# A two-layer trunk in float32r: first transfers, late head norms, a gate tile of its own, a residual in three steps, and one query panel copied out of PSUM

## The chip, the cores and the metric

The kernel runs on one core of one Trainium2 chip. The metric is the device time of one execution in microseconds; lower is better. Three runs of the kernel before took 2197.4, 2202.26 and 2202.55 us, median 2202.26. One execution was profiled: it took 2199.56 us, and its span, first to last recorded instruction, is 2197.8 us.

## The reference

256 tokens of width 2048 go through two layers. Everything is float32.

```python
h = x
u = rms_norm(h, g_a);  q, k, v, fz = split(u @ w_in)          # 3*2048 + 16 gate columns
q, k = rms_norm per head (16 heads of 128)
c = cumsum(log_sigmoid(fz + b_f))                             # per head, over tokens
s = q k^T / sqrt(128) + c[query] - c[key],  causal;  o = softmax(s) v
h = h + o @ w_out
h = h + relu(rms_norm(h, g) @ w1)**2 @ w2                     # 2048 -> 8192 -> 2048
k, v = split(rms_norm(h, g_kv) @ kv_w);  k = rms_norm per head   # shared, computed once
q = rms_norm per head of rms_norm(h, g_b) @ w_q
o = softmax(q k^T / sqrt(128) + relative bias, chunks of 64) v
h = h + o @ w_out
h = h + relu(rms_norm(h, g) @ w1)**2 @ w2
```

## The kernel before

**Weights.** All weight products use float32r. A weight is split into a high part and a remainder, `w = hi + lo` (L142 on ScalarE, L143 on VectorE), the activations likewise, and three products are summed: high by high, high by low, low by high (L319 to L321). The weights come in *units* of 128 x 1024 float32, 512 KB each, which is two contraction blocks of 128 rows by 512 output columns. With two blocks of 128 tokens a unit makes 2 x 2 x 3 = 12 matmuls. Eight units make a *panel*: 512 output columns of all 256 tokens, gathered in a pair of PSUM banks. `ps_acc` holds two such pairs.

The 768 units come in this order: 0 to 95 the input projection (for each of four head groups a q, a k and a v panel), 96 to 127 the output projection, 128 to 383 the MLP in four chunks of hidden columns, 384 to 415 the second layer's q, 416 to 479 the shared k and v, 480 to 511 its output projection, 512 to 767 its MLP. Where a stage is *woven*, its first two panels take turns unit by unit, so that a block of the activations late in the row is needed twice as late.

**Order.** `panels` (L323) runs over the eight units: `fetch` gives a split unit and keeps two more split ahead and up to three raw ones on the way; then come the 12 matmuls; then `run_fill` runs one item of a list named `fill`; and after the last unit the panel's `evac` functions follow, one for each token block. So everything beside the weights is cut into steps, and each step is given a *slot*: the unit after which it is written. `add_fill(items)` adds its n-th item to the n-th slot from now. `keep_order` then fixes the written order on VectorE, ScalarE, TensorE and SyncE, so that a step that waits holds up all that is written behind it on its engine. GpSimd is left free. All transfers are issued by SyncE. A transfer also waits for the one eight before it, since eight semaphores go round among them.

**Turning a panel.** A panel's result has tokens on the partitions, the next product wants them in the free dimension. `blocks32` transposes 32 x 32 blocks on VectorE (L208), and `carry` (L211) puts the rest into DRAM traffic: one store of the rows (`turn<-z`), one empty slot, then four transfers of columns back. Its users: `head_norm`, which squares the accumulator on ScalarE (L347), sums on VectorE (L349), takes a power on GpSimd (L353) and scales out of PSUM on VectorE (L357) before the turn; `turn_hidden` in the MLP, whose `take` does the squared ReLU and the split of one quarter of the hidden activations (L568 to L575); and `next_x`.

**Residual.** `next_x` (L232) ends a panel of an output projection or of the MLP's last chunk. In the evac itself it adds the panel to h on VectorE (L376 or L378), squares the new h on ScalarE with a row sum (`stats.add`, L274), and leaves the turn for the next slot and the carry for the one after; then two steps scale and split the next x (`split_turned`, L188 to L192). These *transitions* lie at 358 to 416 us, 1058 to 1119 us and 1444 to 1506 us. The row statistics are finished by `inverse`, `both` or `flip`, each given a slot after the last panel. The second transition goes to the second layer's q (stage at 1108), and `again` builds a second x in reversed token order for the shared k and v.

**Start.** `begin` (L456) loads x block by block before each of the first panel's units, splits it, loads 8 blocks of h (4 pairs) and squares them, and takes the row roots at the last unit; before the second unit it loads the head gains `hgb` and scales them (L466 to L469). The k panel's slots then hold the two turns of the q panel, `spread` (L295: the row factors as a 128 x 256 tile, by two small matmuls), and `gates` (L482): two steps that each take a buffer of the weight pool's `hi`, clear it on GpSimd (L492), fill it (L495, L496) and make 8 matmuls (L499), then the logs (L503), their store to DRAM and a transpose of the sums. The attention of the group waits for the bias made from that store, for q's columns and for k's; its scores come in the eighth slot of the v panel.

Of the kernel before, what the change touches and what calls it, by code (L numbers as in the profile page):

```python
# [15 lines left out]
P = 128  # L16
# [4 lines left out]
H = 16  # L21
# [26 lines left out]
def trunk(ctx: ExitStack, tc: tile.TileContext, xT, xr, gs, hg, bf, wgate, w_in, w_oa, w1a, w2a,  # L48
# [28 lines left out]
    load_x(0)  # L77
    gsb = const.tile([P, 5 * KT], F32, name="gsb")
    SY.dma_start(gsb, gs)

# [10 lines left out]
    V.memset(mhalf, -0.5)  # L91
    hgb = const.tile([P, 4], F32, name="hgb")
# [139 lines left out]
    def next_x(n, r2, stats, which, into, kept=None):  # L232
# [14 lines left out]
        def f(b, ps):  # L247
            add_h(b, ps)
            stats.add(b, n)
            if b == NB - 1:  # L250
                step = steps(use)
                add_fill([[turn], [lambda: add_fill(carry(*zt) + [[step], [step]])]])
                if kept is not None:
                    kept.append(use)
# [12 lines left out]
    class RowStats:  # L267
# [27 lines left out]
        def spread(self):  # L295
            self.R = const.tile([P, T], F32, name="R")
            pr = ps_o.tile([P, 512], F32, name="pt", tag="po")
            for b in range(NB):
                rb = wk.tile([P, P], F32, name="rb", tag="wk")
                V.tensor_scalar(rb, ones[:, :P], self.r[:, b : b + 1], None, op0=ALU.mult)  # L300
                TE.matmul(pr[:, b * P : (b + 1) * P], rb, ident, start=True, stop=True)
            V.tensor_copy(self.R, pr[:, :T])

# [38 lines left out]
    def head_norm(stats, z, dst):  # L342
        rns = []

        def f(b, ps):
            sq = wk.tile([P, 512], F32, name="sq", tag="wk")
# [3 lines left out]
            vv = sm.tile([P, GH], F32, name="vv")  # L350
            V.tensor_scalar(vv, ss, 1.0 / P, stats().e[:, b : b + 1], op0=ALU.mult, op1=ALU.add)  # L351
            rn = sm.tile([P, GH], F32, name="rn")
            G.tensor_tensor(rn, vv, mhalf, op=ALU.pow)  # L353

            def turn():
                qn = wk.tile([P, 512], F32, name="qn", tag="wk")
                V.tensor_tensor(qn.rearrange("p (a d) -> p a d", a=GH), ps.rearrange("p (a d) -> p a d", a=GH),  # L357
# [3 lines left out]
            rns.append(turn)  # L361
            if b == NB - 1:
                add_fill([[t] for t in rns] + carry(z, dst))
# [57 lines left out]
    def attend(g, q, k, v, cq, o, make_bias, gap):  # L421
# [5 lines left out]
        items[1].append(step)  # L427
        items[4].append(step)
        items[5].append(step)
        for a in range(GH):  # L430
# [25 lines left out]
    def begin(u):  # L456
# [8 lines left out]
        if u == 1:  # L465
            SY.dma_start(hgb, hg)  # L466
            SY.dma_start(bfb, bf)
            V.tensor_scalar(gqk, hgb[:, 0:2], float(P) ** -0.5, None, op0=ALU.mult)
            V.tensor_tensor(gqk, gqk, hgb[:, 2:4], op=ALU.mult)  # L469
        if 2 <= u < 6:  # L470
            for b, n in chunks[2 * u - 4 : 2 * u - 2]:
                c = slice(n * 512, (n + 1) * 512)
                SY.dma_start(h[b][:, c], xr[b][:, c])
        if 4 <= u:
            for b, n in chunks[2 * u - 8 : 2 * u - 6]:
                st0.add(b, n)
        if u == KT // UA - 1:
            st0.roots()

    ct = {}  # L480

    def gates(x, st):  # L482
        wgr = const.tile([P, KT * H], F32, name="wgr")
        r3 = wgr.rearrange("p (k c) -> p k c", k=KT)
        ps = []
        UG = UN // P

        def products(u):
            if u == 0:
                ps.append(ps_s.tile([P, 512], F32, name="s"))  # L490
            w = wsp.tile([P, UN], F32R, name="hi")
            G.memset(w.bitcast(F32), 0.0)  # L492
            w3 = w.rearrange("p (k c) -> p k c", k=UG)
            h3, l3 = w3[:, :, :H], w3[:, :, 32 : 32 + H]
            S.activation(h3, r3[:, u * UG : (u + 1) * UG, :], AF.Copy)  # L495
            V.tensor_tensor(l3, r3[:, u * UG : (u + 1) * UG, :], h3.bitcast(F32), op=ALU.subtract)  # L496
            for j in range(UG):
                k = u * UG + j
                TE.matmul(ps[0], w[:, j * P : (j + 1) * P], x[k], start=k == 0, stop=k == KT - 1)  # L499
# [205 lines left out]
```

## Time and profile before

| | |
|---|---|
| median of three runs | 2202.26 us |
| profiled execution | 2199.56 us |
| its span | 2197.8 us |
| TensorE busy | 2160.6 us, 98% |
| VectorE busy | 1274.4 us, 58% |
| ScalarE busy | 1049.1 us, 48% |
| GpSimd busy | 48.3 us, 2% |
| moved by DMA | 491.60 MB, mean 224 GB/s |
| granted TensorE clock, mean | 0.995 |

In the rows, PE is TensorE's matmul, PEld its weight load, DVE VectorE, ACT ScalarE, POOL GpSimd and SP SyncE. A row of the timeline gives start, duration, engine, line, operation, what it writes and reads, how many were joined, and in brackets how long the engine had been idle and what released it. A matmul of 512 columns is recorded with some 0.39 us, but they are pipelined: what a stretch is worth is seen by how many start in it. In rows of windows the first figure is the window, then the engine's busy time and number of instructions, the granted clock (1.00 is full), the share of the 16 DMA engines and GB/s.

### The profile page before, as it was taken

Reading aid. Unit: us, or ns where it says so; the run is one execution under the profiler, and the core shown is the slowest. Engines: PE = TensorE matmul, PEld = TensorE weight load, DVE = VectorE, ACT = ScalarE, POOL = GpSimd, SP = SyncE. Lnnn points to the kernel's source line nnn. Section 1 sums busy time; section 2 is a strip of 40 time slices with the busy share of each in tenths; the row PEclk is TensorE's granted clock in tenths of the full one; section 3 lists DMA queues with packets and bytes.
Section 4 is the critical chain, followed back from the end, with each engine's and each line's share of the span. In section 5 each row is a group of like instructions: output and inputs, shape, how many; then the busy total and the mean of one; then the engine's idle time right before and its main releaser. Section 6 shows DMA issues by size and latency. Waiting matters only on the chain.

```text
span 2197.8 us, 25786 instructions
## 1 busy us (share of the span) xinstructions
PE 2160.6 (98%) x9514; PEld 1781.1 (81%) x9514; DVE 1274.4 (58%) x1464; ACT 1049.1 (48%) x1251; POOL 48.3 (2%) x48
## 2 busy tenths in 40 slices
PE   7999999999999999999998999999999999999999
PEld 6788888788888888888787888878888888888887
DVE  5677765555555455555566676755555555554554
ACT  5545444554344344345564444455543543443443
POOL 0000000000000000000001000000000000000000
PEclk9999999999999999999999999999999999999999
DMA  7676777786686577577677777767866765865774
GB/s 257 209 253 208 241 256 225 223 250 215 194 250 211 193 240 227 192 230 231 204 235 220 245 229 233 237 198 240 265 202 205 237 213 194 252 212 192 239 225 167
DMA packets 183887, 491.60 MB, mean 224 GB/s; under 512 B 36929, under 2 KB 73937, under 8 KB 183761
## 3 DMA queue, kind: packets, MB, share of 16 engines
q1 hardware_dynamic: 183760, 489.96, 70.4%
q8 instruction: 74, 1.21, 0.2%
q14 instruction: 53, 0.43, 0.1%
HBM read 450.01 MB, written 39.87 MB: 223 GB/s over the span
## 4 chain that ended last, share of the span: by engine, by line
PE 91%; DMA 3%; ACT 2%; DVE 2%; issue 1%; SPq 0%; POOL 0%; DVEq 0%; ACTq 0%; POOLq 0%
PE acc L320 30%; PE acc L321 30%; PE acc L319 30%; DMA raw<-in_w_in 1%; ACT hi L142 1%; DMA turn<-z 1%; DVE lo L143 1%; PE po L415 1%; PE s L384 1%; DMA raw<-in_w_ob 0%; DMA raw<-in_w_oa 0%; ACT act L191 0%; DMA raw<-in_w2a 0%; ACT z L188 0%; PE po L416 0%
## 5 line engine op out<-in xcount | busy, mean ns | idle before, releaser
L143 DVE TENSOR_TENSOR lo<-raw,hi 128x1024 fp32r<-128x1024 f32 (+1 forms) x770 | 936.7, 1218 | 810.5 <-ACT hi L142 802.9
L142 ACT ACTIVATE hi<-raw 128x1024 fp32r<-128x1024 f32 (+1 forms) x770 | 811.7, 1057 | 1002.9 <-PE acc L321 960.5
L319 PE MATMUL acc<-hi,act 128*128 128x512 f32 x3072 | 1210.1, 394 | 15.3 <-DVE qn L357 7.4
L320 PE MATMUL acc<-lo,act 128*128 128x512 f32 x3072 | 1201.1, 391 | 7.7 <-DVE lo L143 7.7
L321 PE MATMUL acc<-hi,act 128*128 128x512 f32 x3072 | 1199.7, 391 | 0.8 <-DVE act L180 0.8
L319 PEld LDWEIGHTS acc<-hi,act 128*128 128x128 f32 x3072 | 579.3, 189 | 137.8 <-ACT hi L142 10.0
L320 PEld LDWEIGHTS acc<-lo,act 128*128 128x128 f32 x3072 | 579.3, 189 | 133.1 <-DVE lo L143 14.5
L321 PEld LDWEIGHTS acc<-hi,act 128*128 128x128 f32 x3072 | 578.8, 188 | 122.6 <-DVE act L180 2.0
L353 POOL TENSOR_TENSOR rn<-vv,mhalf 128x4 f32<-128x4 f32 x32 | 42.7, 1349 | 432.7 <-DVE vv L351 432.7
L208 DVE STREAM_TRANSPOSE z<-acc 128x512 f32<-128x512 f32 x64 | 42.0, 696 | 11.8 <-PE acc L321 11.8
L418 ACT ACTIVATE act<-po 128x256 fp32r<-128x256 f32 x32 | 12.3, 385 | 69.4 <-PE po L416 69.4
L575 DVE TENSOR_TENSOR act<-q,act 128x1024 fp32r<-128x1024 f32 x32 | 39.0, 1219 | 0.0
L572 ACT ACTIVATE act<-q 128x1024 fp32r<-128x1024 f32 x32 | 34.0, 1062 | 1.0
L568 ACT ACTIVATE q<-q 128x1024 f32<-128x1024 f32 x32 | 33.4, 1045 | 0.6 <-DMA q<-turn 0.6
L574 ACT ACTIVATE q<-q 128x1024 f32<-128x1024 f32 x32 | 33.3, 1042 | 0.0
L188 ACT ACTIVATE z<-q,gsb 128x256 f32<-128x256 f32 x64 | 28.7, 496 | 5.9 <-DMA q<-turn 3.1
L419 DVE TENSOR_TENSOR act<-po,act 128x256 fp32r<-128x256 f32 x32 | 13.5, 423 | 30.7 <-ACT act L418 30.7
L274 ACT ACTIVATE sqr<-h 128x512 f32<-128x512 f32 x32 | 19.9, 624 | 22.3 <-DVE h L376 14.0
L349 DVE TENSOR_REDUCE ss<-sq 128x4 f32<-128x512 f32 x32 | 21.8, 681 | 14.2 <-ACT sq L347 14.2
L401 ACT ACTIVATE pr<-t,nm 128x128 f32<-128x128 f32 x64 | 28.4, 446 | 1.6 <-DVE nm L398 1.0
L378 DVE SCALAR_TENSOR_TENSOR h<-acc,qn,h 128x512 f32<-128x512 f32 x32 | 22.6, 747 | 11.0 <-PE acc L321 11.0
L192 DVE TENSOR_TENSOR act<-z,act 128x1024 fp32r<-128x1024 f32 x16 | 19.6, 1226 | 10.4 <-ACT act L191 10.4
(96 smaller groups left out, 427.9 us busy)
## 6 DMA issues: line engine op xcount, KB each, us to landing
raw<-in_w1a SPq DMA_DIRECT2D x128, 512.0 KB, 4.0
raw<-in_w2a SPq DMA_DIRECT2D x128, 512.0 KB, 3.6
raw<-in_w1b SPq DMA_DIRECT2D x128, 512.0 KB, 4.2
raw<-in_w2b SPq DMA_DIRECT2D x128, 512.0 KB, 3.7
raw<-in_w_in SPq DMA_DIRECT2D x94, 512.0 KB, 4.4
raw<-in_w_kv SPq DMA_DIRECT2D x64, 512.0 KB, 4.3
turn<-z SPq DMA_DIRECT2D x60, 512.0 KB, 4.1
q<-turn SPq DMA_DIRECT2D x176, 128.0 KB, 5.9
```

The costliest lines, as they stand in the source:

```text
L142: S.activation(hi[:, c], raw[:, c], AF.Copy)
L143: V.tensor_tensor(lo[:, c], raw[:, c], hi[:, c].bitcast(F32), op=ALU.subtract)
L188: S.activation(y[:, j].rearrange("p (b i c) -> p b i c", b=NB, i=4), t[:, j], AF.Copy, scale=gsb[:, m : m + 1])
L208: V.transpose(z.rearrange("p (j n b c) -> p b n j c", j=4, n=n, b=nb)[:, b], src.rearrange("p (n j c) -> p n j c", n=n, j=4))
L319: TE.matmul(ps[b], xh, wh, start=k == 0, stop=False)
L320: TE.matmul(ps[b], xh, wl, start=False, stop=False)
L321: TE.matmul(ps[b], xl, wh, start=False, stop=k == KT - 1)
L353: G.tensor_tensor(rn, vv, mhalf, op=ALU.pow)
L568: S.activation(t, t, AF.Relu)
L572: S.activation(hi, t, AF.Square)
L574: S.activation(t, t, AF.Square)
L575: V.tensor_tensor(lo, t, hi.bitcast(F32), op=ALU.subtract)
```

## The change

The diff changes six things:

- The gains `gs` are loaded ahead of the first block of x, and a square of a small constant is the first work of ScalarE.
- `begin` loads one block of h per unit from the fourth unit on and squares one from the sixth on; the rest goes to slots of the k panel, with the roots. The head gains, the gate bias and the gate weights are loaded at the k panel's start (`head_gains`).
- `head_norm` has two new options. With `late` the norms' own steps go to a slot given by it (6 for the first q panel, so slot 5, and the turns to 6 and 7). With `copied` each half is first copied out of PSUM (first q panel of the second layer), and the turn reads the copy.
- The gate weights get a tile of the activation pool, cleared in slot 0, filled in slot 2 and used in slots 3 and 4; `spread` is in two steps, slots 5 and 6, and the gates' logs follow in slots 7, 8 and 9, the transpose in slot 12.
- `next_x` leaves the squares to the first slot, the turn to the second, and has an empty slot ahead of its two split steps; what follows from the statistics moves by one slot, and `again` by two more.
- The hidden quarters' two steps come two slots later, and the bias steps one.

```diff
@@ -76,5 +76,5 @@
 
-    load_x(0)
     gsb = const.tile([P, 5 * KT], F32, name="gsb")
     SY.dma_start(gsb, gs)
+    load_x(0)
 
@@ -91,2 +91,4 @@
     V.memset(mhalf, -0.5)
+    first = sm.tile([P, GH], F32, name="first", bufs=1)
+    S.activation(first, mhalf, AF.Square)
     hgb = const.tile([P, 4], F32, name="hgb")
@@ -248,6 +250,6 @@
             add_h(b, ps)
-            stats.add(b, n)
             if b == NB - 1:
                 step = steps(use)
-                add_fill([[turn], [lambda: add_fill(carry(*zt) + [[step], [step]])]])
+                add_fill([[lambda b=b: stats.add(b, n) for b in range(NB)], [turn],
+                          [lambda: add_fill(carry(*zt) + [[], [step], [step]])]])
                 if kept is not None:
@@ -297,7 +299,10 @@
             pr = ps_o.tile([P, 512], F32, name="pt", tag="po")
+            rb = wk.tile([P, NB, P], F32, name="rb", tag="wk")
             for b in range(NB):
-                rb = wk.tile([P, P], F32, name="rb", tag="wk")
-                V.tensor_scalar(rb, ones[:, :P], self.r[:, b : b + 1], None, op0=ALU.mult)
-                TE.matmul(pr[:, b * P : (b + 1) * P], rb, ident, start=True, stop=True)
+                V.tensor_scalar(rb[:, b], ones[:, :P], self.r[:, b : b + 1], None, op0=ALU.mult)
+            yield
+            for b in range(NB):
+                TE.matmul(pr[:, b * P : (b + 1) * P], rb[:, b], ident, start=True, stop=True)
             V.tensor_copy(self.R, pr[:, :T])
+            yield
 
@@ -341,6 +346,10 @@
 
-    def head_norm(stats, z, dst):
-        rns = []
+    def head_norm(stats, z, dst, late=0, copied=False):
+        rest = []
 
         def f(b, ps):
+            src = ps
+            if copied:
+                src = wk.tile([P, 512], F32, name="qc", tag="wk")
+                V.tensor_copy(src, ps)
             sq = wk.tile([P, 512], F32, name="sq", tag="wk")
@@ -349,6 +358,8 @@
             V.tensor_reduce(ss, sq.rearrange("p (a d) -> p a d", a=GH), axis=AX.X, op=ALU.add)
-            vv = sm.tile([P, GH], F32, name="vv")
-            V.tensor_scalar(vv, ss, 1.0 / P, stats().e[:, b : b + 1], op0=ALU.mult, op1=ALU.add)
             rn = sm.tile([P, GH], F32, name="rn")
-            G.tensor_tensor(rn, vv, mhalf, op=ALU.pow)
+
+            def norm():
+                vv = sm.tile([P, GH], F32, name="vv")
+                V.tensor_scalar(vv, ss, 1.0 / P, stats().e[:, b : b + 1], op0=ALU.mult, op1=ALU.add)
+                G.tensor_tensor(rn, vv, mhalf, op=ALU.pow)
 
@@ -356,3 +367,3 @@
                 qn = wk.tile([P, 512], F32, name="qn", tag="wk")
-                V.tensor_tensor(qn.rearrange("p (a d) -> p a d", a=GH), ps.rearrange("p (a d) -> p a d", a=GH),
+                V.tensor_tensor(qn.rearrange("p (a d) -> p a d", a=GH), src.rearrange("p (a d) -> p a d", a=GH),
                                 rn.unsqueeze(2).to_broadcast([P, GH, P]), op=ALU.mult)
@@ -360,5 +371,7 @@
 
-            rns.append(turn)
+            rest.append((norm, turn))
+            if not late:
+                norm()
             if b == NB - 1:
-                add_fill([[t] for t in rns] + carry(z, dst))
+                add_fill([[]] * (late - 1) + ([[n for n, _ in rest]] if late else []) + [[t] for _, t in rest] + carry(z, dst))
         return f
@@ -426,5 +439,5 @@
         step = steps(lambda: make_bias(g, box))
-        items[1].append(step)
-        items[4].append(step)
+        items[2].append(step)
         items[5].append(step)
+        items[6].append(step)
         for a in range(GH):
@@ -464,17 +477,22 @@
             x.append(split_x(raw_x[u][:, j], u * UA + j, 0))
-        if u == 1:
-            SY.dma_start(hgb, hg)
-            SY.dma_start(bfb, bf)
-            V.tensor_scalar(gqk, hgb[:, 0:2], float(P) ** -0.5, None, op0=ALU.mult)
-            V.tensor_tensor(gqk, gqk, hgb[:, 2:4], op=ALU.mult)
-        if 2 <= u < 6:
-            for b, n in chunks[2 * u - 4 : 2 * u - 2]:
-                c = slice(n * 512, (n + 1) * 512)
-                SY.dma_start(h[b][:, c], xr[b][:, c])
-        if 4 <= u:
-            for b, n in chunks[2 * u - 8 : 2 * u - 6]:
-                st0.add(b, n)
-        if u == KT // UA - 1:
-            st0.roots()
-
+        if u >= 3:
+            rows_in(u - 3)
+        if u >= 5:
+            st0.add(*chunks[u - 5])
+
+    def rows_in(i):
+        b, n = chunks[i]
+        c = slice(n * 512, (n + 1) * 512)
+        SY.dma_start(h[b][:, c], xr[b][:, c])
+
+    def head_gains():
+        SY.dma_start(hgb, hg)
+        SY.dma_start(bfb, bf)
+        SY.dma_start(wgr, wgate)
+        yield
+        V.tensor_scalar(gqk, hgb[:, 0:2], float(P) ** -0.5, None, op0=ALU.mult)
+        V.tensor_tensor(gqk, gqk, hgb[:, 2:4], op=ALU.mult)
+        yield
+
+    wgr = const.tile([P, KT * H], F32, name="wgr")
     ct = {}
@@ -482,19 +500,20 @@
     def gates(x, st):
-        wgr = const.tile([P, KT * H], F32, name="wgr")
         r3 = wgr.rearrange("p (k c) -> p k c", k=KT)
-        ps = []
-        UG = UN // P
-
-        def products(u):
-            if u == 0:
-                ps.append(ps_s.tile([P, 512], F32, name="s"))
-            w = wsp.tile([P, UN], F32R, name="hi")
+        w = acts.tile([P, 2, GH, T], F32R, name="act")
+        w3 = w.rearrange("p i a t -> p (i a t)").rearrange("p (k c) -> p k c", k=KT)
+        box = []
+
+        def clear():
             G.memset(w.bitcast(F32), 0.0)
-            w3 = w.rearrange("p (k c) -> p k c", k=UG)
+
+        def parts():
             h3, l3 = w3[:, :, :H], w3[:, :, 32 : 32 + H]
-            S.activation(h3, r3[:, u * UG : (u + 1) * UG, :], AF.Copy)
-            V.tensor_tensor(l3, r3[:, u * UG : (u + 1) * UG, :], h3.bitcast(F32), op=ALU.subtract)
-            for j in range(UG):
-                k = u * UG + j
-                TE.matmul(ps[0], w[:, j * P : (j + 1) * P], x[k], start=k == 0, stop=k == KT - 1)
+            S.activation(h3, r3, AF.Copy)
+            V.tensor_tensor(l3, r3, h3.bitcast(F32), op=ALU.subtract)
+
+        def products(ks):
+            if not box:
+                box.append(ps_s.tile([P, 512], F32, name="s"))
+            for k in ks:
+                TE.matmul(box[0], w3[:, k], x[k], start=k == 0, stop=k == KT - 1)
 
@@ -505,5 +524,5 @@
             u = wk.tile([H, T], F32, name="gu", tag="wk")
-            S.activation(z, ps[0][:H, T:], AF.Copy)
-            V.tensor_tensor(u, ps[0][:H, :T], z, op=ALU.add)
-            S.activation(z, ps[0][32 : 32 + H, :T], AF.Copy)
+            S.activation(z, box[0][:H, T:], AF.Copy)
+            V.tensor_tensor(u, box[0][:H, :T], z, op=ALU.add)
+            S.activation(z, box[0][32 : 32 + H, :T], AF.Copy)
             V.tensor_tensor(u, u, z, op=ALU.add)
@@ -532,5 +551,5 @@
 
-        step = steps(logs)
-        return ([[lambda: SY.dma_start(wgr, wgate)], []] + [[lambda u=u: products(u)] for u in range(KT // UG)]
-                + [[step], [step], [step], [], [turn_c]])
+        step, spread = steps(logs), steps(st.spread)
+        return [[clear], [], [parts], [lambda: products(range(8))], [lambda: products(range(8, KT))], [spread], [spread],
+                [step], [step], [step], [], [], [turn_c]]
 
@@ -552,6 +571,12 @@
         qb = {}
-        panels(x, [head_norm(lambda: st0, zq, lq)], begin if g == 0 else None)
-        add_fill([[]] * 7 + [[lambda qb=qb, lq=lq: qb.update(q=scale_q(lq, 0))]])
+        late = 6 if g == 0 else 0
+        panels(x, [head_norm(lambda: st0, zq, lq, late)], begin if g == 0 else None)
         if g == 0:
-            add_fill([[st0.spread]] + gates(x, st0))
+            step = steps(head_gains)
+            add_fill([[step], [], [], [], [step]])
+            add_fill([[lambda i=i: rows_in(i)] for i in range(5, 8)])
+            add_fill([[lambda i=i: st0.add(*chunks[i])] for i in range(3, 8)])
+            fill[4].insert(len(fill[4]), st0.roots)
+            add_fill(gates(x, st0))
+        add_fill([[]] * (7 + late) + [[lambda qb=qb, lq=lq: qb.update(q=scale_q(lq, 0))]])
         zk, k = turned("k")
@@ -587,3 +612,3 @@
                         step = steps(lambda: take(zt[1]))
-                        add_fill(carry(*zt) + [[step], [step]])
+                        add_fill(carry(*zt) + [[], [], [step], [step]])
                 return f
@@ -595,3 +620,3 @@
     stage(o, [next_x(n, None, st1, 1, x1) for n in range(NG)], True)
-    add_fill([[], [], [st1.inverse]])
+    add_fill([[], [], [], [st1.inverse]])
     st2, xb, kept = RowStats("b"), [], []
@@ -600,3 +625,3 @@
     again = [steps(lambda n=n: kept[n](True, 2, xkv)) for n in range(NG)]
-    add_fill([[], [st2.both], [], [st2.flip]] + [[]] * 6 + [[again[i // 2]] for i in range(2 * NG)])
+    add_fill([[], [], [st2.both], [], [st2.flip]] + [[]] * 8 + [[again[i // 2]] for i in range(2 * NG)])
 
@@ -607,6 +632,6 @@
 
-        def f(b, ps, box=box):
+        def f(b, ps, box=box, g=g):
             if b == 0:
                 z, lq = turned("z")
-                box["lq"], box["f"] = lq, head_norm(lambda: st2, z, lq)
+                box["lq"], box["f"] = lq, head_norm(lambda: st2, z, lq, copied=g == 0)
             box["f"](b, ps)
@@ -639,3 +664,3 @@
     stage(o, [next_x(n, None, st3, 4, x3) for n in range(NG)], True)
-    add_fill([[], [], [st3.inverse]])
+    add_fill([[], [], [], [st3.inverse]])
 
```

## The prediction

> **What bounds the kernel now.** I read the page first, then busy time by window, then the waits of PE, and last the timeline around each place that loses time. From the page:
>
> ```profile
> span 2197.8 us, 25786 instructions
> ```
> ```profile
> PE 2160.6 (98%) x9514; PEld 1781.1 (81%) x9514; DVE 1274.4 (58%) x1464; ACT 1049.1 (48%) x1251; POOL 48.3 (2%) x48
> ```
>
> PE is the bound. Where it falls short shows by window (us, PE busy and its matmuls, granted clock, DMA share, GB/s):
>
> ```profile
> 6.57:35.23 28.66, 25.02 (x97) 1.00 0.96 344
> 35.23:71.56 36.33, 29.56 (x118) 0.91 0.44 141
> 358.00:416.00 58.00, 54.49 (x228) 0.97 0.73 220
> 388.73:392.14 3.41, 3.41 (x9) 0.50 0.43 148
> 440.00:1040.00 600.00, 600.00 (x2649) 1.00 0.70 222
> 1058.00:1119.00 61.00, 57.31 (x241) 0.97 0.69 214
> 1147.00:1175.00 28.00, 20.61 (x85) 0.88 0.48 163
> 1444.00:1506.00 62.00, 57.70 (x242) 0.97 0.70 212
> ```
>
> The 600 us stretch is the full pace: 600/2649 = 0.2265 us a matmul, 2.72 us a weight unit of 12. Loss is a window less its matmuls at that pace. First panel (q, 96 matmuls): 28.66 - 21.74 = 6.9 us. Second (k): 96 + 16 gate matmuls are 25.4, and with 0.8 for the spread 10.1 are lost. The three windows at 358, 1058 and 1444 hold the residual transitions: 6.4, 6.4 and 7.2. The window at 1147 (second layer's q panels): 8.75. Together 46 us; the MLP loses nothing. What PE waited for (total, times, longest):
>
> ```profile
> PE acc L320 <- DVE lo L143: 7.7, 11, 2.2
> PE acc L319 <- DVE qn L357: 7.4, 1, 7.4
> PE acc L319 <- ACT hi L142: 7.2, 7, 2.0
> PE s L499 <- DVE hi L496: 3.5, 2, 1.7
> PE pt L301 <- DVE rb L300: 3.3, 1, 3.3
> ```
>
> All five lie in those places; the change touches each.
>
> **Part 1: start and first panel.**
>
> ```profile
> 3.80 1.28 ACT L179 ACT_TABLE_LOAD   x1 [3.80 <-DMA gsb<-in_gs]
> ```
> ```profile
> 11.85 1.06 ACT L142 ACTIVATE hi<-raw 128x1024 fp32r<-128x1024 f32 x1 [0.36 <-DMA raw<-in_w_in]
> ```
> ```profile
> 12.68 0.17 DVE L468 TENSOR_SCALAR gqk<-hgb 128x2 f32<-128x2 f32 x1 [3.33 <-DMA hgb<-in_hg]
> ```
> ```profile
> 13.71 0.50 PE L320 MATMUL acc<-lo,act 128*128 128x512 f32 x1 [2.20 <-DVE lo L143]
> ```
> ```profile
> h<-in_xr SPq DMA_DIRECT2D x8, 256.0 KB, 6.7
> ```
>
> The table load waits for gsb, then 1.28 us go before the first split. The new `first` square loads the table while the transfers run, and gsb goes ahead of the first x block, so the first matmul moves from 6.57 to about 5.5. DVE stands 3.33 us at L468 in front of a weight split; PE pays 2.20 of it. With hgb in the k panel the next thing late is the raw of the third unit, landing at 11.85: that unit starts near 13.1. After it the transfers set the pace (344 GB/s, share 0.96). Only 2 or 3 instead of 6 blocks of h go ahead of the seventh unit's weights: 262144 B at 344 GB/s is 0.76 us, four of them 3.0. ACT also does 3 squares instead of 8 there. The panel's end gains 3.0 by the flow alone, 4.7 if the earlier start carries through. I take 4; ends 2 (the flow bites earlier) and 6 (nearly all that is lost).
>
> **Part 2: the k panel.**
>
> ```profile
> 53.20 0.95 POOL L492 MEMSET hi<- 128x1024 f32 x1 [13.75 <-PE acc L321]
> ```
> ```profile
> 54.88 2.11 PE L499 MATMUL s<-act,hi 128*128 128x512 f32 x8 [1.74 <-DVE hi L496]
> ```
> ```profile
> 57.03 1.06 ACT L142 ACTIVATE hi<-raw 128x1024 fp32r<-128x1024 f32 x1 [2.53 <-PE s L499]
> ```
>
> The 10.1 fall into three parts. Spread's factors stand on DVE behind both head norms: 3.3 of waiting. After that pause PE runs at less than full clock (0.91 over 36.33 us: 3.3). Each of the two gate products takes a weight buffer, so POOL's clearing waits for matmuls (13.75 in its row), ACT and DVE follow, and PE waits 3.5 in all; the next weight split then waits 2.53 for the products. Afterwards the tile is one of the `act` pool, cleared and filled slots before the products in slots 3 and 4; the norms wait to slot 5 and the spread goes in two steps around its matmuls. No wait remains on this chain. What is late next: the rows of h and their squares now run into slot 4, beside POOL's roots; and the first panel's PSUM pair comes free only at the turn in slot 7, which I put 0.4 after the v panel wants it. If that cover is gone (h rows late, roots slip), 3 to 4 return. Taken: 9.7, ends 6 and 10.
>
> **Part 3: what part 2 pushes into the v panel.** Two norms' turns, gate logs, their store and the transposes of c now fall into its first five slots.
>
> ```profile
> 71.56:94.24 22.68, 22.68 (x104) 18.58 (x102) 16.73 (x23) 10.59 (x12) 2.76 (x2) 1.00 0.84 279
> ```
> ```profile
> 65.83 0.41 DVE L507 TENSOR_TENSOR gu<-s,gz 16x256 f32<-16x256 f32 x1
> ```
> ```profile
> 84.75 1.75 SPq L224 DMA_DIRECT2D k<-turn  x4
> ```
> ```profile
> k<-turn SPq DMA_DIRECT2D x32, 128.0 KB, 4.9
> ```
> ```profile
> 93.77 0.38 PE L383 MATMUL s<-k,q 128*128 128x128 f32 x2
> ```
>
> The busy figures are PE, PEld, DVE, ACT and POOL: DVE has 16.73 of 22.68 us. Gate steps near 0.41 each and a turn add some 4, all in the first five slots of 13.6. Laid end to end in the written order (turn, five gate steps, two reduces, a split; then the scan, a turn of k, a split; the store's copies, the other turn, a split) the weight splits of the panel's third to fifth unit come 0.4, 1.0 and 0.4 late: 2. On SP the store, the q columns, the k rows and the bias queue ahead of the k columns. These are issued 13.2 after the panel's start now (84.75 - 71.56), and the last lands some 4.9 after its issue near 86.0, at 90.9: 2.9 before the scores at 93.77. Behind k's turn at about 11.7 the rows are issued at 13 and land some 4.7 later (near the columns' 4.9), so the columns go at 17.7 to 19.5 and land at 24, where the scores want them at 23.6: up to 1. Taken: -3, ends -7 and -1.
>
> **Part 4: residual in three steps.**
>
> ```profile
> 386.48 0.50 PE L319 MATMUL acc<-hi,act 128*128 128x512 f32 x1 [1.50 <-ACT hi L142]
> 387.75 0.50 PE L320 MATMUL acc<-lo,act 128*128 128x512 f32 x1 [0.76 <-DVE lo L143]
> ```
> ```profile
> 1062.62 0.63 ACT L274 ACTIVATE sqr<-h 128x512 f32<-128x512 f32 x1 [3.14 <-DVE h L378]
> ```
> ```profile
> 1063.91 2.94 ACT L142 ACTIVATE hi<-raw 128x1024 fp32r<-128x1024 f32 x3
> ```
>
> ACT stands 3.14 us at a square until DVE has added the second half, and 1.3 in the squares; the weight split queued behind makes PE wait twice (1.50, 0.76). Put into the next unit's slot, the squares run behind that split. The turn goes one slot later, the y steps two: the last quarter of x is ready around slot 10, needed at 12, and the inverse is moved with it. What is late next is DVE's add itself, about 0.5 a panel end. The three places lose 20.0; I leave 2, so 18. Ends: 9 (the split's lo still late) and 20.
>
> The row at 388.73 is a window of 3.41 us at clock 0.50 after waits of only 1.50 and 0.76; it costs half of itself, 1.7. So I let a leftover of some 2 us at the copied place (next part) take the clock down once. The Trainium skill, "TensorE: Matmul & The Clock Gate", Part 1, says that half rate returns only after a whole idle window of about 3.4 us. By that rule no drop would follow there, and the sum would be 1.7 better, 31.9; the trace disagrees.
>
> **Part 5: the copied panel.**
>
> ```profile
> 1154.24 1.06 ACT L347 ACTIVATE sq<-acc 128x512 f32<-128x512 f32 x2
> ```
> ```profile
> 1151.05 0.69 DVE L349 TENSOR_REDUCE ss<-sq 128x4 f32<-128x512 f32 x1 [0.72 <-ACT sq L347]
> ```
> ```profile
> 1159.66 0.68 DVE L357 TENSOR_TENSOR qn<-acc,rn 128x512 f32<-128x512 f32 x1
> ```
> ```profile
> 1164.71 0.71 DVE L208 STREAM_TRANSPOSE z<-qn 128x512 f32<-128x512 f32 x1 [3.04 <-DMA turn<-z]
> ```
> ```profile
> 1147.00:1175.00 28.00, 20.61 (x85) 16.62 (x85) 20.20 (x27) 15.27 (x22) 5.40 (x4) 0.88 0.48 163
> ```
>
> The third panel waits 7.39 for the last read of the first one's PSUM. Copies of 0.68 each free it, but in the built order every square waits for its half's copy, and the second copy stands behind the first's reduce: 0.68 + 0.53 + 0.69 + 0.2 + 0.68 + 0.53 = 3.3 us, begun some 1.2 late behind a quarter's lo, against 2.72 of cover by the woven partner: 1.8 remain. The copies add 1.4 to DVE, and the flipped x of the next stage now falls into the same slots, so splits of the next two units come 1.7 and 2.5 late; the z buffer can still wait for its store (3.04 in the row). 1.8 + 1.7 + 2.5 make 6.0, with one clock drop 7.7 at most; I leave 7.2 of the 8.75: 1.5. Ends: -2 (the 3.04 comes on top) and 7 (DVE keeps up, 20.20 busy of 28.00 before).
>
> The Trainium skill, "PSUM — Partial Sum Buffer", Terms, says that two engines must not access one bank at once, reads against reads included, which speaks against a copy beside a square. By that rule the order above has to stand; without it the panel would come free some 1.2 us sooner and the sum be 31.4. No run here shows a collision.
>
> **Part 6: hidden quarters.** Their splits come two slots (5.44 us) later in eight stages.
>
> ```profile
> 512.15 1.22 DVE L575 TENSOR_TENSOR act<-q,act 128x1024 fp32r<-128x1024 f32 x1
> ```
> ```profile
> 525.76 0.39 PE L319 MATMUL acc<-hi,act 128*128 128x512 f32 x1
> ```
>
> The last quarter is done at 513.4 and first read at 525.76: 12.4 spare, then 6.9. Cost 0, as is bias one slot later.
>
> **Sum:** 4 + 9.7 - 3 + 18 + 1.5 = 30.2 faster. The profiled execution took 2199.56, so 2169.4; it was 2.7 below the median of 2202.26 (runs from 2197.4), so the new median may stand up to 2.7 above its profile; with half of it, 2171.
>
> **Rivals.**
> - Transitions half cured: DVE's add, one turn and splits still collide, as the 0.76 row warns. Gain 9 there: 2180.
> - The v panel pays 8 more: k columns behind rows, bias and two weights on SP, with a clock drop. The scores are 2.9 us from their columns now. 2179.
> - The copy pays in full, DVE keeping up: 5.5 to 7 more, 2165. For it: PE's 7.4 had one cause. Against it: DVE's 20.20 busy of 28.00 before two copies and the flipped x come in.
> - It does little: the start is bound by transfers anyway, a new wait stands where each old one did, and 5 to 8 are left: 2195.
> - Slower: hidden quarters come too late. The place is the tenth slot of the eight stages on w2, the price the lateness beyond 6.9 us spare. It turns the sign at 30.2/8 = 3.8 a stage, or 10.7 past now; at 5 a stage 40 are lost, 2211. Against it: the row from 440 has the transfers at share 0.70 and PE without a gap, so nothing there runs late now.
>
> **How the numbers follow.** Forecast 0.53 (its own range 2163 to 2178), half cured 0.15, v panel 0.12, copy 0.06, little 0.05, slower 0.09. The range from 2160 to 2190 leaves out the last two, 0.14. Within 0.3% (6.6 us, about what a measurement can tell from no change) I count "little" as a whole; the first four are all faster, 0.86.
>
> **What would show it.** First matmul before 6 us; no 3.3 us wait in front of L468's heir; no memset of a weight buffer and no PE wait at the gate products; windows of the transitions at one matmul per 0.23 us; clock 1.00 in them. Wrong if PE waits over 3 us at the v panel's end for k, over 5 at the copied panel's successor for splits, or at all in the w2 stages.

## The result

The changed kernel took 2173.67 us (median of 4 runs, 2171.72 to 2181.28), the kernel before 2199.83 (4 runs, 2193.81 to 2202.55). The ratio is 0.9891, with a 95% interval from 0.9857 to 0.9925. The profiled execution took 2172.02 us. From the page after:

```profile
span 2169.8 us, 25773 instructions
```
```profile
PE 2151.4 (99%) x9514; PEld 1776.5 (82%) x9514; DVE 1280.5 (59%) x1465; ACT 1048.8 (48%) x1251; POOL 48.4 (2%) x47
```

Windows of PE after the change, over the same work as the windows shown of before (us, busy and matmuls, granted clock, DMA share, GB/s):

```profile
5.75:30.05 24.30, 24.30 (x96) 1.00 1.01 381
30.05:56.05 26.00, 26.00 (x117) 1.00 0.61 200
56.05:81.76 25.71, 23.70 (x103) 1.00 0.76 249
350.00:402.00 52.00, 52.00 (x231) 1.00 0.84 252
410.00:1010.00 600.00, 600.00 (x2648) 1.00 0.70 221
1044.00:1100.00 56.00, 55.32 (x245) 1.00 0.81 244
1127.00:1154.00 27.00, 22.44 (x90) 0.94 0.49 168
1147.13:1150.55 3.42, 3.42 (x10) 0.50 0.84 283
1424.00:1480.00 56.00, 56.00 (x249) 1.00 0.83 253
```

At 0.2265 us a matmul the second row has nothing left of its 10.1 us of loss, and the transitions (350, 1044, 1424) keep 0, 0.5 and 0 of 20.0. The copied place (1127) still loses 6.6 of 8.75. The v panel (56.05) takes 25.71 where it took 22.68. What PE waited for after:

```profile
PE s L396 <- DMA k<-turn: 4.7, 4, 2.0
PE acc L325 <- DVE lo L145: 3.4, 4, 1.9
PE acc L324 <- ACT sq L356: 2.3, 1, 2.3
```

The five waits shown of before are gone but for a part of the splits. The first row is new: scores that wait for their key columns, four times. To set gain against forecast, take the start of every weight unit in both traces and see by how much the lead changes from one to another (up to the start of the last unit; the spans differ by 28.0):

| stretch (units) | forecast | measured |
|---|---|---|
| start and first panel (to 8) | 4 | 5.2 |
| k panel (8 to 16) | 9.7 | 10.3 |
| v panel of the first group (16 to 24) | -3 | -3.0 |
| later groups' attention (24 to 96) | 0 | -4.6 |
| three transitions (112 to 132, 368 to 388, 496 to 516) | 18 | 6.6 + 5.9 + 7.5 = 20.0 |
| copied panel (399 to 405) | 1.5 | 2.0 |
| second layer's k and v (440 to 480) | 0 | -1.5 |
| everything else, MLP included | 0 | -0.6 |
| sum | 30.2 | 27.8 |

### The profile page after: what moved, and what is told of

The parts are those of the page before. It is cut to its first block, busy times and chain, and to the rows that moved or that the text cites. A ratio compares the mean times of both kernels' runs of the same rounds, so it can differ in the third digit from the quotient of the medians.

```text
span 2169.8 us, 25773 instructions
## 1 busy us (share of the span) xinstructions
PE 2151.4 (99%) x9514; PEld 1776.5 (82%) x9514; DVE 1280.5 (59%) x1465; ACT 1048.8 (48%) x1251; POOL 48.4 (2%) x47
## 4 chain that ended last, share of the span: by engine, by line
PE 92%; DMA 4%; DVE 2%; ACT 1%; SPq 1%; issue 1%; DVEq 0%; ACTq 0%
PE acc L325 30%; PE acc L324 30%; PE acc L326 30%; DMA k<-turn 1%; DMA turn<-z 1%; DVE lo L145 1%; PE s L397 1%; PE po L428 1%; ACT hi L144 1%; SPq L226 0%; DMA prT<-turn 0%; PE s L396 0%; DMA raw<-in_w2a 0%; DVE qn L368 0%; PE po L429 0%
## 5 line engine op out<-in xcount | busy, mean ns | idle before, releaser
L593 ACT ACTIVATE q<-q 128x1024 f32<-128x1024 f32 x32 | 33.4, 1044 | 0.0
L391 DVE SCALAR_TENSOR_TENSOR h<-acc,qm,h 128x512 f32<-128x512 f32 x32 | 22.6, 747 | 5.5 <-PE acc L326 5.5
```

The lines of the kernel that those rows point to most:

```text
L391: V.scalar_tensor_tensor(hc, ps, r2[:, b : b + 1], hc, op0=ALU.mult, op1=ALU.add)
L593: S.activation(t, t, AF.Relu)
```

## The experiments

The first question was the loss that the sum did not have: attention behind the first group.

**a_bias: the bias steps back in slots 1, 4 and 5.**

```diff
-        items[2].append(step)
-        items[5].append(step)
-        items[6].append(step)
+        d = 1 if cq is not None and g == 0 else 0
+        items[1 + d].append(step)
+        items[4 + d].append(step)
+        items[5 + d].append(step)
```

> The changed kernel with one part undone: the bias steps stand in slots 1, 4 and 5 of the v panel again, except for the first head group, where they stay one slot later. In the changed kernel the last key columns of the second head group land 24.8 us after the start of its k panel's successor instead of 20.0, and PE waits for them. Theory: the bias transfer, 768 KB, and two weight units now stand between the key rows and the key columns in the DMA queues, so the columns land late in all six later groups; with the bias back ahead of the rows the stretch from the second group to the end of the first layer's attention gains 4.6 us and the second layer's 1.5, so the profiled span falls from 2169.8 to about 2163.7. Rival: the columns are late because all transfers come in another phase since the start is faster; then the span stays within 1 us of 2169.8 and PE still waits for the key columns by over 3 us in all.

Units 24 to 96 lose 0.5 instead of 4.6, units 440 to 480 lose 0.1 instead of 1.5. PE's waits for key columns:

```profile
PE s L396 <- DMA k<-turn: 2.3, 1, 2.3
```

One is left, the first group's, whose bias had not moved. So 5.5 us of the loss are the bias step, and the rival falls. Why, the DMA issues of SP show, of the kernel before, of the changed kernel and of this one, in the second group, whose v panel starts at 142.21, 129.77 and 131.74 us (start, time to issue, queue, line, what, how many):

```profile
157.71 1.76 SPq L224 DMA_DIRECT2D k<-turn  x4
```
```profile
138.87 0.33 SPq L220 DMA_DIRECT2D turn<-z  x1
139.24 1.51 SPq L559 DMA_DIRECT2D bias<-cd  x1
140.86 1.17 SPq L134 DMA_DIRECT2D raw<-in_w_in  x2
143.81 2.08 SPq L226 DMA_DIRECT2D k<-turn  x4
```
```profile
140.53 0.33 SPq L220 DMA_DIRECT2D turn<-z  x1
141.63 2.17 SPq L134 DMA_DIRECT2D raw<-in_w_in  x2
146.87 1.75 SPq L226 DMA_DIRECT2D k<-turn  x4
```

In the kernel before and in this one the bias went out ahead of the rows, 4.2 and 4.3 us after the panel's start. One slot later its 768 KB stand between the rows' store and the columns. In the changed kernel the columns are issued earlier, 14.0 us after the panel's start instead of 15.5 as before, since the store lands sooner (at 14.0 instead of 15.5); but the last of them lands 24.8 after it, where it landed at 20.0 before and lands at 21.2 in `a_bias`. The expectation speaks of six later groups; the edit moves the step in seven, three in the first layer and four in the second, where the bias is 512 KB. The span is 2167.9, not the 2163.7 expected: the first panel gave 1.3 less, and 3.1 more were lost near unit 536, where this execution's weights landed up to 10 us after their issue. The median is 2169.47, the ratio to before 0.9866 (0.985 to 0.9881); that interval overlaps the changed kernel's, so the step's worth is told by its stretches.

**b_res, c_copy, d_start, n_gate: parts alone, on the kernel before.** `b_res` has the residual in three steps with what moves along; `c_copy` the copied panel; `d_start` all that concerns the first head group; `n_gate` only the gate tile. Their edits are the hunks of the diff above; of `c_copy`, for one:

```diff
-                box["lq"], box["f"] = lq, head_norm(lambda: st2, z, lq)
+                box["lq"], box["f"] = lq, head_norm(lambda: st2, z, lq, copied=g == 0)
```

> The kernel before with the residual in three steps alone (squares, turn and carry in slots of their own, two empty slots, the row statistics and the second reading of x moved with them). Theory: the three transitions lose nothing more, 19 to 20 us, so the span goes from 2197.8 to about 2178.5, and no other stretch changes by over 1 us. Rival: part of the gain seen in the transitions came from work that the other parts had moved (the copied panel, the later hidden quarters); then a transition keeps more than 1.5 us of its loss and the span stays above 2183.

Measured: span 2175.0, ratio 0.9914 (0.9898 to 0.9929). The transitions gain 5.6, 6.9 and 7.2, together 19.7. Most of the rest of its lead (3.35 us by unit 16) lies in the k panel, 2.85 us, where this execution's clock stayed up although the code there is the old one. The theory holds: the transitions needed no other part of the change.

> The kernel before with the copied panel alone. Theory: the wait of 7.4 us for the last read of PSUM goes, the third panel starts about 2 to 2.5 us late behind copy, square, copy, square, and the splits behind VectorE's longer work lose some 3 to 4 us later, with one drop of the clock; the stretch of the second layer's q panels gains 1 to 3 us, and the span stands near 2196. Rival: the copy alone is worth the whole wait, 5 to 7 us, and it is the later place of the second reading of x that eats the gain in the changed kernel; then the span stands near 2191.

Measured: span 2196.3, ratio 1.0 (0.9991 to 1.0009). The lead grows by 7.9 at units 400 and 401 and shrinks by 8.4 at 403 and 404, so the copy alone gains nothing. The theory's place is right and its sum 1.5 to 3.5 us too kind; the rival falls. The 8.4 are in the main two waits of PE for the split's remainder, 2.3 each, and two half-clock windows, where the theory had one. These waits had been 7.7, 11, 2.2 in all:

```profile
PE acc L320 <- DVE lo L143: 12.7, 13, 2.3
```

The splits are late for two reasons. Ahead of the first VectorE has no gap from 1156 us on. Ahead of the second it stands still, until a z buffer's store has landed:

```profile
1165.75 0.71 DVE L208 STREAM_TRANSPOSE z<-qn 128x512 f32<-128x512 f32 x1 [3.20 <-DMA turn<-z]
```

The kernel before has the same wait (3.04) at 1164.71; there PE was so late already that the units behind it lost nothing.

> The kernel before with the changes to the start alone: order of the first transfers, thinner loading of h, late norms of the first q panel, the gate tile, the spread in two steps, and the first group's bias one slot later. Theory: the first panel ends 5.2 us earlier, the k panel gains 10.3 and the v panel gives 3.0 back, so the span stands 12.5 lower, near 2185.3, and nothing changes behind the first group. Rival: the 3 us given back in the v panel are answered by later groups as well, because the transfers stay behind; then the loss goes on growing after the first group and the span stands above 2188.

Measured: span 2192.8, ratio 0.9964 (0.9952 to 0.9977). The k panel gains 10.3 again, but the first panel only 3.6, and the v panel gives 7.0 back up to unit 25 instead of 3.0. The span lies where the rival had it, but not for its reason, and the theory's sum misses: behind the first group the attention loses only 0.6 more, and the extra is a wait of 3.8 for the first group's key columns and one half-clock window. (The three transitions, with the old code, differ by 1.4 in all from the trace of before.) In the eight traces with this same code in that place the columns land 25.0 to 28.0 us after the v panel's start, and the panel gives back 3.1 to 8.0: the term has a size of its own in each execution.

> The kernel before with one part alone: the gate weights in a tile of the activation pool, loaded and cleared in slot 0 of the k panel, filled in slot 2, used in slots 3 and 4; the head norms and the spread stay as before. Theory of the prediction: the k panel's 10.1 us fall into 3.3 of waiting for the spread, 3.3 of half clock after it, and about 3.5 in front of the two gate products; so the units from 11 to 13 gain 3.5 to 4.2 us and the wait for the spread stays (3.3), units 8 to 10 unchanged within 0.5. Rival: the gate steps wait because they stand behind the spread's pause, and without late norms the tile gains under 2 us.

Measured: the two units with the gate products gain 4.07. The kernel was run once; its span is 2190.2. The other 3.5 of its 7.6 us lie in the first panel (1.3), in several places away from the edit, and in units 8 to 10 (1.2, where at most 0.5 was expected): behind the wait for the spread the clock was down for one window here and for two in the trace of before. The wait before the gate products is gone, and the rival falls. The wait for the spread stays:

```profile
PE pt L301 <- DVE rb L300: 3.3, 1, 3.3
```

So of the 10.3 in the k panel 4.1 are the gate tile; the other 6.2 are left for the late norms with the two-step spread, which were not run alone, and for the clock that no longer falls.

**e_sq, f_y: what is left at the copied place.** These two and `i_hid5` were run once each, so they are read by their stretches alone. PE and ScalarE in the changed kernel:

```profile
1135.29 0.50 PE L324 MATMUL acc<-hi,act 128*128 128x512 f32 x1 [2.30 <-ACT sq L356]
```
```profile
1146.82 0.91 ACT L190 ACTIVATE z<-q,gsb 128x256 f32<-128x256 f32 x2 [5.08 <-DMA turn<-z]
```

The `e_sq` edit:

```diff
-            S.activation(sq, ps, AF.Square)
+            S.activation(sq, src, AF.Square)
```

> The changed kernel with one edit: in the copied panel the squares read the copy instead of PSUM, so that the pair is free after the two copies. In the changed kernel PE waits 2.30 us for the second square there. Theory: that wait falls to 0.5 or less, because both copies can run back to back once VectorE is free, and the stretch from weight unit 399 to 405 (2.0 us better than before now) gains another 1 to 2; what follows is bound by VectorE, which is hardly idle from 1130 to 1148 us, so a part of it comes back as later splits. Rival: nothing of the wait returns later and the whole 2.3 us are gained.

```profile
1136.68 0.47 PE L324 MATMUL acc<-hi,act 128*128 128x512 f32 x1 [1.80 <-DVE qc L354]
```

The wait falls by 0.5 only, and units 399 to 405 gain 0.8; theory and rival both miss. The copies are not back to back: the evac is written block by block, so the first half's sum, which waits for its square, stands between them.

`f_y` takes y from another ring:

```diff
-        y = qkv.tile([P, GH * T], F32, name="z").rearrange("p (k t) -> p k t", k=GH)
+        y = qkv.tile([P, GH, REL], F32, name="bias").rearrange("p a r -> p (a r)")[:, : GH * T].rearrange("p (k t) -> p k t", k=GH)
```

> The changed kernel with one edit: the scaled panel y of split_turned takes a buffer of the idle bias ring instead of the z ring. In the changed kernel ScalarE stands 5.08 us at its first y of the flipped x, until the store of a turned query panel has landed, with a weight split behind it, and unit 404 starts 3.73 us late. Theory of the prediction (the z buffer's wait on top of VectorE's work): the 5.08 us wait goes, unit 404 starts 1 to 3 us earlier, and at most 2.7 us are lost there. Rival: VectorE alone sets these starts, the wait of ScalarE was hidden behind it; then units 403 to 405 start within 0.5 us of the changed kernel's.

The 5.08 us wait is gone, and the step to unit 404 falls from 6.45 to 3.96 us, so the z ring did cost, and of the 3.73 us that unit 404 was late 1.2 are left, within the theory. Units 399 to 405 gain only 1.6, since the clock fell earlier in this execution (at 1139.3). Then units 405 to 416 gave 1.6 back, so that by unit 416 nothing is left of the gain.

**i_hid5: the margin of the hidden quarters.**

```diff
-                        add_fill(carry(*zt) + [[], [], [step], [step]])
+                        add_fill(carry(*zt) + [[]] * 5 + [[step], [step]])
```

> The changed kernel with five empty slots instead of two ahead of the hidden quarter's two steps, so that each quarter is split 8.2 us later still. This measures the margin on which the prediction's slower case rests (6.9 us left in the changed kernel). Theory: the last quarter is now 1.3 us late in each of the eight stages on the second MLP matrix, and with the split queued behind it 1 to 2 us are lost in each: 8 to 16 us in all, nowhere else. Rival: weight units ready ahead hide it, the quarter is late by less than they cover, and under 3 us are lost in all.

```profile
PE acc L326 <- DVE act L600: 5.2, 8, 0.6
```

Eight waits, one in each stage, at the thirteenth unit, where the last quarter is first read, and 0.97 us of the lead in each: 7.8 in all, a little under the theory's 8; the rival falls. This fits the margin as it was read: a quarter that by it comes 1.3 us late costs 1.0.

**g_best and k_g0bias: a version from these readings.** `g_best` is the changed kernel with a_bias, e_sq and f_y, and with the norms and turns of the second layer's first two query panels put off:

```diff
-                box["lq"], box["f"] = lq, head_norm(lambda: st2, z, lq, copied=g == 0)
+                box["lq"], box["f"] = lq, head_norm(lambda: st2, z, lq, late=(3, 4, 0, 0)[g], copied=g == 0)
...
-                add_fill([[]] * 7 + [[lambda: qs.append(scale_q(box["lq"], 1))]])
+                add_fill([[]] * (7 + (3, 4, 0, 0)[g]) + [[lambda: qs.append(scale_q(box["lq"], 1))]])
```

> A version after the readings so far: the changed kernel with the bias steps in slots 1, 4 and 5 for all but the first head group, the copied panel's squares reading the copy, the flipped x scaled into a buffer of the bias ring, and the norms and turns of the first two query panels of the second layer 3 and 4 slots later, so that VectorE's work between units 400 and 405 is spread. Expected: 5.5 us from the bias (4 in the first layer, 1.5 in the second), 4 to 6 of the 6.7 us still lost between units 399 and 405; together about 10 below the changed kernel, a profiled span near 2160. If VectorE's total work over the stage is the limit and not its place, the second term is under 2 us.

Measured: median 2165.1, span 2164.5, ratio 0.9849 (0.9836 to 0.9862). Units 399 to 405 gain 5.1 on the changed kernel, of which 1.3 return by 416, and no half-clock window came there. By the expectation's sign it was the place of VectorE's work and not its amount; but the later norms were not run without `e_sq` and `f_y`, which alone gained 0.8 and 1.6 in these units, so 2.7 of the 5.1 are theirs by subtraction. The bias gives its share (5.7). The v panel of the first group takes 3.5 of it back. `k_g0bias` turns to that:

```diff
+        at = (4, 7, 7) if cq is not None and g == 0 else (1, 4, 5)
+        for i in at:
+            items[i].append(step)
```

> The best version so far with one more edit: in the first head group the bias is fetched in slot 4 of the v panel, behind the key columns, and both of its additions stand in slot 7, ahead of the scores. In the traces so far the first group's key columns are issued 17 to 19 us after the v panel's start and land 25 to 29 after it, behind the bias of 768 KB and two weight units, while the scores want them at 23.6; the v panel gives 3 to 8 us back. Theory: without the bias ahead the columns land 2 to 3 us sooner and PE's wait for them falls below 1.5 us; VectorE's additions then wait for the bias, which costs up to 1.5 us of splits, so the stretch from unit 16 to 25 gains 2 to 4 us against the version before and the span falls to about 2161.5. Rival: the two weight units are what is in the way; then the columns gain under 1 us and the additions' wait makes the stretch longer.

The wait for the key columns, first in `g_best` (where the profile puts it down to a ScalarE step that had long been done), then here:

```profile
PE s L396 <- ACT v L455: 3.4, 1, 3.4
```
```profile
PE s L396 <- DMA k<-turn: 0.6, 1, 0.6
```

Units 16 to 25 gain 4.4. Median 2162.78, span 2159.6, ratio 0.9839 (0.9822 to 0.9856). The last columns land 24.0 us after the panel's start instead of 26.9, with the two weight units still ahead of them. So it is the bias that was in the way, as in the later groups.

**l_defer and m_both.**

```diff
+            if not copied:
+                total()
...
             def norm():
+                if copied:
+                    total()
```

`total` is the sum of squares on VectorE, `V.tensor_reduce(ss, sq, ...)`.

> The best version so far with one more edit: in the copied panel the two sums of squares on VectorE move from between the copies to the slot of the norms, so that the second copy stands directly behind the first. With the squares reading the copy PE still waited 1.54 to 1.80 us for the second copy, since the first half's sum, which waits for its square on ScalarE, stood between the copies. Theory: that wait falls to 0.2 or less and the stretch from unit 399 to 405 gains 1 to 1.5 us. Rival: the copies come late because VectorE is still at a split of x when the panel ends; then at least 0.8 us of the wait stays.

```profile
PE acc L324 <- ACT sq L356: 0.2, 1, 0.2
```

The wait for PSUM is gone, 1.3 of it stay to unit 405 and 0.9 to unit 416. The median is 2166.84 (ratio 0.986, 0.9843 to 0.9878), no better than `g_best`'s 2165.1, and the intervals overlap. In the profiled execution the first v panel gave 1.5 more back than in `g_best`'s trace; the other executions have no trace.

> Both last edits together on the best version: the first group's bias behind its key columns, and the two sums of squares of the copied panel in the slot of the norms. Each was measured alone against the version without either: the first moved the first group's wait for the key columns from 3.4 to 0.6 us (span 2159.6), the second the wait at the copied panel from 1.5 to 0.2, of which about 0.9 stayed. Theory: they add, the span falls to about 2158.7 and the median to 2162. Rival: the first layer's start and transfers vary by more than that from run to run, so nothing can be told between this version and the one with the first edit alone.

Measured: median 2161.47 (5 runs, 2160.65 to 2162.69), span 2158.9, ratio to before 0.9833 (0.9814 to 0.9853). They add in the trace (0.9 at the copied place). Against `k_g0bias` by itself the medians are 1.3 apart and the intervals overlap, so the second edit's worth is told by its stretch alone. Against the changed kernel, 2173.67, it is 12 us, and the intervals of their ratios to before are apart.

## Why the prediction was right

The time lay where it was forecast, 2173.67 against 2171, and the profiled span of 2169.8 against a sum that gave 2169.4 for the whole execution, which took 2172.02. Part of that closeness is luck, twice. Terms too small by 4.3 in all stood against one of 6.1 that was missing. And over the eight traces with the same code up to unit 25 the three terms of the start come to 6.3 to 12.5 us together, 8.5 in the mean, for a forecast of 10.7; the execution profiled for the result is the 12.5.

- *First panel* (4 taken, 5.2 measured, 3.3 to 5.2 over the ten traces with that start). The third unit starts 2.6 sooner, as the raw weights' landing set it. From there the flow decides, as said, and varies.
- *k panel* (9.7, measured 10.3). The three causes were read rightly; `n_gate` gives 4.1 for the gate part against 3.5 in the waits. But the clock's 3.3 belonged to the one execution that was read: with the same wait for the spread the clock fell for two windows there, for one in `c_copy` and `n_gate`, for none in `b_res`, and the panel took 36.3 us, 35.1 in `c_copy` and 33.5 in `b_res`.
- *v panel* (-3, measured -3.0 in the profiled run). Issue of the key columns at 17.4 to 18.8 and landing at 25.0, for a forecast of 17.7 to 19.5 and 24. PE waited 1.55 for them. But the profiled execution was a kind one: of the eight traces five give back 6.6 to 8.0, near or past the end of -7, with the columns late behind bias and weights and a clock drop, much as that rival had it. In six of the eight PE waits over 3 us there for k, which the prediction had named as a sign of being wrong.
- *Transitions* (18, measured 20.0). The 2 us left for VectorE's add did not come; the windows keep 0.5 us in the second and nothing in the others. `b_res` shows the part by itself (19.7), and "half cured" falls. With the old code the three places together differ by -1.4 to 2.0 us from the trace of before (`d_start`, `c_copy`, `n_gate`), which is small against 20.
- *Copied panel* (1.5, measured 2.0). PE waits 2.30 for the second square where 1.8 was worked out; the z ring, which I had put at the range's end, was real (5.08 on ScalarE), and the splits of two units came late. `c_copy` says that alone the copy gains nothing: behind the wait that it covers stood VectorE's dense work and a wait for the z ring, at nearly the same times as before.
- *Hidden quarters* (0, measured -0.1 and -0.4 in the two MLPs, at single units and not stage by stage). `i_hid5` bears out the margin and a price of 1 us a stage. The slower case would have needed far more.
- *Bias one slot later* (0; the stretches behind the first group gave -6.1, of which `a_bias` puts 5.5 down to this step). This is the step that failed: "Cost 0, as is bias one slot later." The edit was judged by when the bias is used, and in the seven later groups VectorE never waits for it. What it moves past on SP was not counted: 768 KB change places with the rows that the key columns need. In the first group I had counted exactly that; the same order in the other seven groups was left out.

On the clock: one half window at the copied place was allowed for, and one came, at 1147.13. The Trainium skill's rule of a whole idle window ("TensorE: Matmul & The Clock Gate", Part 1) would have had none; the window ahead of it held 2.14 us of idle time out of 3.41, so here the trace disagrees.

## What to carry to other kernels

A transfer that is moved can cost by what it is moved in front of, even if its own use is hidden: for every moved transfer, list the latency chains (store, landing, fetch back) in whose middle it now stands. A copy that freed a buffer early gained nothing here while the copying engine had no slack at that place and stood behind a wait of its own; look at its row in that stretch, at work and waits, and put off what nobody needs soon. Where several terms are summed, compare term by term afterwards, since a good total can hide a missing one.

## What the runs showed of the hardware

The granted clock falls by a threshold, not by a whole idle window. In each trace the half-clock windows start on one grid of 3.413 us: the five falls in the trace of before, over 1437 us, agree within 0.002 us. I added up PE's idle time (gaps between starts less 0.2265) in the window just ahead of each fall. In the 12 traces with a fall all 28 followed a window with 2.04 us or more idle, some 60%, and only five of these windows were idle throughout. No window at full clock with 2.0 us or less idle led to a fall. Between 2.02 and 2.10 two windows did and seven did not; above that every one did.

A fall lasts one window or two at 0.50, so it costs 1.7 us, or 3.4 where PE has work all the time. The wait of 2.30 us in the changed kernel, cut in two by the grid (1.95 idle in the fuller window), went free, and the one behind unit 403, with 2.14 in one window, did not. Where the grid lies in the span differs from trace to trace, so the same wait can cost or not: the wait of 3.3 us for the spread, with the same code, put 2.63 to 3.07 us into one window in three traces, which fell, and at most 1.93 in `b_res`, which did not.

The first layer's transfers vary too. With the same code the key columns of the first group landed between 25.0 and 28.0 us after their panel's start, and PE waited 1.55 to 4.55 us for them.
